# A two-layer attention trunk on one core: a second place for P of the selected branch, shared with the split G rows, and new prices in the planner that orders the second layer

## The chip, the core and the metric

The kernel runs on one core of a Trainium2 chip. Engines are named as the profile names them: PE is TensorE's matmul stream and PEld its weight loads, DVE is VectorE, ACT is ScalarE, POOL is GpSimd, SP is SyncE, which here issues nearly all DMAs. Each engine takes its own instructions in the order in which they were written, and waits for others through semaphores. The metric is the device time of one execution in microseconds.

## The reference, cut to what matters

```
x = x + swa(x)                 # layer A: 16 heads, window of 128 keys, sinks
shared K/V from x              # three branches: compressed, selected, window
q = rms(proj), z = proj        # layer B: 4 KV heads, 4 query heads in each
o_cmp = softmax(q k_cmp + bias) v_cmp
o_slc = softmax(q k_slc + bias, the 8 selected blocks of 64 keys) v_slc
o_win = softmax(q k_win + bias, window of 512 keys) v_win
G = sum over branches of o_b * silu(z_b) * sigmoid(gate_b)
out = x + G @ w_out
```

Sequence 1024, width 1024, all float32. The products with weights are made of float32r parts: an operand is split into a high part and the rest, and three products replace one.

## The kernel before, in words

Layer A takes the first 440 us, the shared K/V side, the queries and a part of z the next 500, and from about 940 us to the end runs what this text calls the second attention, written by `plan_b`. Its work is cut into 32 units: for each of four **quads** h (one KV head, four query heads) eight tiles i of 128 queries. Unit (i, h) makes, in this order, compressed scores (`sc_b`), window scores (`s_wb`, against up to 5 blocks of 128 keys) and selected scores (`s_sb`, up to i+1 blocks). DVE adds the bias to them while it copies them from PSUM into P (`p_wb`, `p_sb`) and takes row maxima, ACT takes the exponential in place, PE transposes P block by block (`pt_wb`, `pt_sb`), ACT or DVE copies each transposed block back, and PE multiplies it with V into `o_b`. One transposition of the row scales (`rt_b`) ends the softmax part of a unit; it serves below as the mark between units. The result goes to DRAM (`gdb`) and is read back, all quads of one tile, for the output rows (`gs`: high part and rest, 8 KB each for a partition), which `op` multiplies with `w_out`.

The products with V are **half-width**: they write 64 of the 128 output rows (shown as `128*64`), two of them side by side. All others are full-width.

Two kinds of product depend on nothing in the units and fill PE between their steps: z of the quads 1 to 3 (`z_b`, 127 groups of three 512-column products) and, once all quads of a tile are there, the output products (`op`, 128 such groups).

The order is not written by hand. Each step is an operation with an engine, a price in microseconds, a due time and the buffers it takes from rings of fixed depth; `Plan.run` picks the operation that could start first by its own prices, and so fixes every engine's order. A change of a price or of a ring moves instructions on all engines. A ring that an operation needs is a wait in the real kernel too: with `psl=1` there is one place for `p_sb`, so unit i+1 can put no selected scores away before the last product with V of unit i has read its P. Here are the lines that say how a half-width product is priced:

```
if (j + 1) * runs // n > j * runs // n:      # up to five blocks in a run
    last = plan.op("PE", 0.15 + 0.45 * len(js), ..., kind="half")
new = o["kind"] != kind.get(e)               # Plan.run: another kind than before
start = max(at, free) + self.change * new    # change: 0 in plan_b, 0.12 in plan_a
```

## Time and profile before

| | us |
|---|---|
| median of three runs (1549.99 to 1554.86) | 1550.21 |
| the profiled execution | 1548.54 |
| its span, first to last instruction | 1546.6 |
| PE busy | 1497.1 (97%) |
| PEld busy | 1202.2 (78%) |
| DVE busy | 949.7 (61%) |
| ACT busy | 784.3 (51%) |
| POOL busy | 335.2 (22%) |

Busy times of PE overlap, since products are pipelined: a 512-column product is shown with 0.39 us, and the next one starts 0.23 us later. What a stretch costs is read from starts, not from durations.

### The profile page before, as it was taken

The numbers are of one execution on the slowest core, as the hardware profiler recorded it, in microseconds if no ns is written. First come the engines' busy times: TensorE is split into PE (matmuls) and PEld (weight loads), VectorE is DVE, ScalarE is ACT, GpSimd is POOL, SyncE is SP. The second block draws the span as 40 slices with busy tenths as digits, with TensorE's granted clock in tenths as the row PEclk, the third lists the DMA queues.
The fourth block names the chain that finished last, engine by engine and source line by source line (L and its number), as shares of the span: only waits on it lengthen the run. The fifth ranks groups of instructions, "written<-read, shape, count | busy, mean of one in ns | idle before, by whom it ended". The sixth has DMA issues, their size and how long they took to land.

```text
span 1546.6 us, 26037 instructions
## 1 busy us (share of the span) xinstructions
PE 1497.1 (97%) x8579; PEld 1202.2 (78%) x8579; DVE 949.7 (61%) x3801; ACT 784.3 (51%) x1874; POOL 335.2 (22%) x417
## 2 busy tenths in 40 slices
PE   7999989999989999999999999999999999999999
PEld 5778867677768888898788887777787787668777
DVE  7678625857646544588524428875887786777431
ACT  6322315867525343242423427776777786766530
POOL 1233101211101000234100002332332342353200
PEclk9999999999999999999999999999999999999999
DMA  6365685644345323454825534334324333453132
GB/s 211 103 198 137 176 223 156 205 127 150 118 159 156 105 79 112 129 144 112 222 78 153 142 97 116 111 102 141 114 84 147 109 105 105 148 154 97 32 128 87
DMA packets 194506, 203.87 MB, mean 132 GB/s; under 512 B 22095, under 2 KB 154914, under 8 KB 194372
## 3 DMA queue, kind: packets, MB, share of 16 engines
q1 hardware_dynamic: 172368, 189.50, 41.5%
q10 hardware_dynamic: 21124, 10.49, 2.4%
q0 software_dynamic: 880, 2.23, 0.5%
q8 instruction: 68, 1.11, 0.3%
q14 instruction: 66, 0.54, 0.1%
HBM read 147.41 MB, written 56.85 MB: 132 GB/s over the span
## 4 chain that ended last, share of the span: by engine, by line
PE 80%; DVE 7%; DMA 7%; issue 2%; ACT 2%; POOL 1%; SPq 0%; POOLq 0%; DVEq 0%; ACTq 0%
PE o_b L962 7%; PE bkv L366 5%; PE pt_sb L953 4%; PE s_sb L1641 4%; PE op L864 4%; PE op L866 4%; PE op L865 4%; PE z_b L435 3%; PE z_b L434 3%; PE z_b L433 3%; PE s_wb L1641 3%; PE c L366 3%; PE pt_wb L953 3%; PE akv L366 2%; PE z_b L724 2%
## 5 line engine op out<-in xcount | busy, mean ns | idle before, releaser
L1016 ACT ACTIVATE p_sb<-p_sb,negm_sb 128x128 f32<-128x128 f32 (+7 forms) x128 | 98.8, 774 | 10.8 <-DVE negm_sb L1678 10.0
L1016 ACT ACTIVATE p_wb<-p_wb,negm_wb 128x640 f32<-128x640 f32 (+4 forms) x128 | 88.7, 695 | 21.9 <-DVE negm_wb L1678 21.2
L957 ACT COPY p_sb<-pt_sb 128x512 f32<-128x512 f32 x143 | 78.1, 587 | 41.9 <-PE pt_sb L953 41.5
L1641 PE MATMUL s_sb<-k,q_b 128*128 128x384 f32 (+3 forms) x384 | 96.6, 367 | 2.5 <-DVE mx_sb L1669 1.7
L435 PE MATMUL z_b<-xt_b,w_bz 128*128 128x512 f32 x240 | 93.9, 391 | 0.0
L434 PE MATMUL z_b<-xt_b,w_bz 128*128 128x512 f32 x240 | 93.8, 391 | 0.0
L433 PE MATMUL z_b<-xt_b,w_bz 128*128 128x512 f32 x240 | 93.7, 390 | 0.0
L673 DVE SCALAR_TENSOR_TENSOR zt_b<-zt_b,z_b 128x512 f32<-128x512 f32 x48 | 32.8, 685 | 93.9 <-ACT zt_b L670 93.8
L366 PE MATMUL bkv<-w_bkv,xt_b 128*128 128x512 f32 x336 | 85.8, 409 | 4.3 <-ACT w_bkv L315 2.8
L1641 PE MATMUL s_wb<-k,q_b 128*128 128x384 f32 (+3 forms) x384 | 85.6, 333 | 3.2 <-issue 2.7
L957 ACT COPY p_wb<-pt_wb 128x512 f32<-128x512 f32 x120 | 67.9, 582 | 35.6 <-PE pt_wb L953 34.8
L1006 POOL TENSOR_TENSOR uz_b<-uz_b,rb_b 128x512 f32<-128x512 f32 x32 | 42.0, 1312 | 198.0 <-DMA rb_b<-rdb 164.3
L953 PE MATMUL pt_sb<-consts,p_sb 128*128 128x128 f32 x576 | 79.8, 275 | 1.7 <-ACT p_sb L957 1.1
L953 PEld LDWEIGHTS pt_sb<-consts,p_sb 128*128 128x128 f32 x576 | 65.4, 141 | 17.7 <-issue 10.0
L366 PEld LDWEIGHTS bkv<-w_bkv,xt_b 128*128 128x128 f32 x336 | 64.5, 196 | 18.8 <-ACT w_bkv L315 3.2
L670 ACT ACTIVATE zt_b<-z_b 128x512 f32<-128x512 f32 x48 | 28.5, 596 | 91.7 <-PE z_b L435 72.6
L1006 POOL TENSOR_TENSOR uz_a<-uz_a,rb_a 128x256 f32<-128x256 f32 x32 | 26.0, 813 | 224.5 <-DMA rb_a<-rda 179.6
L1016 ACT ACTIVATE p_a<-p_a,negm_a 128x256 f32<-128x256 f32 (+1 forms) x128 | 61.8, 484 | 25.2 <-DVE negm_a L1257 15.2
L875 DVE TENSOR_TENSOR xo<-op,xo 128x512 f32<-128x512 f32 x32 | 22.1, 689 | 85.3 <-PE op L866 82.5
L962 PE MATMUL o_b<-p_sb,v 128*64 128x256 f32 x576 | 72.8, 390 | 0.0
L1660 DVE CUSTOM_DVE_ANT_1 p_sb<-s_sb,sel_b 128x256 f32<-128x256 f32 (+3 forms) x128 | 56.6, 453 | 25.0 <-PE s_sb L1641 18.7
L1641 PEld LDWEIGHTS s_sb<-k,q_b 128*128 128x128 f32 x384 | 62.5, 191 | 11.1 <-issue 3.6
(377 smaller groups left out, 4332.1 us busy)
## 6 DMA issues: line engine op xcount, KB each, us to landing
ws_bz<-in_b_w_in_dram SPq DMA_DIRECT2D x24, 512.0 KB
uz_b<-uzb SPq DMA_DIRECT2D x32, 384.0 KB
qda<-qs_aq SPq DMA_DIRECT2D x64, 128.0 KB
q_a<-qda SPq DMA_DIRECT2D x32, 256.0 KB
qdb<-qs_bq SPq DMA_DIRECT2D x64, 128.0 KB
q_b<-qdb SPq DMA_DIRECT2D x32, 256.0 KB
rb_b<-rdb SPq DMA_DIRECT2D x64, 128.0 KB
uzb<-zt_b ACTq DMA_DIRECT2D x30, 256.0 KB
```

What stands on the lines that cost most here:

```text
L366: mm(c["ps"], x, w(z, k), start=start and n == 0, stop=stop and n == len(ops) - 1)
L433: mm(ps, wh, xh, start=(k == 0), stop=False)
L434: mm(ps, wl, xh, start=False, stop=False)
L435: mm(ps, wh, xl, start=False, stop=(k == KC - 1))
L864: mm(u["ps"], gh, wh, start=(k == 0), stop=False)
L865: mm(u["ps"], gh, wl, start=False, stop=False)
L953: nc.tensor.transpose(t[:, g * P : (g + 1) * P], p()[:, g, cols], self.ident)
L957: nc.scalar.copy(p()[:, :, cols], t) if e == "ACT" else nc.vector.tensor_copy(p()[:, :, cols], t)
L962: nc.tensor.matmul(o()[z * HD : (z + 1) * HD], v()[:, blocks[j], :], p()[:, z::2, j * P : (j + 1) * P], start=(j == 0), stop=(j == n - 1),)
L1006: nc.gpsimd.tensor_tensor(u(), u(), c["b"], op=ALU.mult)
L1016: self.nc.scalar.activation(p[:, g, :n], p[:, g, :n], AF.Exp, bias=negm[:, g : g + 1], accum_out=sums[:, g : g + 1])
L1641: nc.tensor.matmul(s["s"][:, : nbk * P], cq(g), k[:, y, (b0 + at) * P : (b0 + at + nbk) * P], start=(y == 0), stop=(y == 1),)
```

## The change

P of the selected branch gets a second ring. Units with odd i keep the old place (`psl`), units with even i take a new one (`pev`) of the same 16 KB. The room for it is the room of the two `gs` buffers: both have the tag `both` with one buffer, so the first output rows can be split only when the last even unit has used its P; the plan lists all `pev` operations ahead of the loads of the G rows. Each of the two halves of this room then holds the G rows of one tile, by turns. The ring `uz` (z and gates of a unit) grows from 2 to 3. The prices: a change between half-width and full-width costs 0.18 in both plans, a run of half-width products 0.432 for each block instead of 0.15 + 0.45, a group of z or output products 0.69 instead of 0.66, scores a little more, and an operation of another kind is held back by 0.1 (`keep`) in `plan_b`.

```
-  0.66, product(k)                                   # z and output products
+  0.69, product(k)
-  "PE", 0.15 + 0.45 * len(js), ... times(js)         # plan_pv
+  "PE", 0.432 * len(js), ... times(js)
-  plan.change, plan.keep = 0.12, 0.15                # plan_a
+  plan.change, plan.keep = 0.18, 0.15
-  a = first = plan.op("PE", n / 600.0, scores(j), ...
+  a = first = plan.op("PE", n / 530.0, scores(j), ...
-  a = plan.op("PE", 2 * nbk * 0.054, scores(g, at, nbk, s), ...
+  a = plan.op("PE", 0.025 + 2 * nbk * 0.054, scores(g, at, nbk, s), ...
-  ... uz=2, ... psl=1, zt=2, gs=2, ...               # plan_b
+  ... uz=3, ... psl=1, pev=1, zt=2, gs=2, ...
+  def even():
+      return pool.tile([P, GRP, 1024], F32, tag="both", name="p_sb", bufs=1)
+  def part(i):
+      if not parts:
+          parts["g"] = pool.tile([P, 2, 2, SLOT], F32R, tag="both", name="gs", bufs=1)
+      return parts["g"][:, i % 2]
-  far_win if b else far_sel, None if b else fop, "pw" if b else "psl", 640 if b else 1024, prio,
+  far_win if b else far_sel, None if b else fop, "pw" if b else "psl" if i % 2 else ("pev", even),
+  ends = [o for o in plan.ops if any(b["ring"] == "pev" for b in o["bufs"])]
-  lo = self.plan_split(lambda: gd[i], KC, rows, gops, [gb], [], p, f"g{i}", 2.8)
+  lo = self.plan_split(lambda: gd[i], KC, rows, gops + (place[1] if place else []), [gb], [], p, f"g{i}", 2.8)
+  plan.change, plan.keep = 0.18, 0.1                 # plan_b
```

How the order moves on PE is seen at three places. In names of rows, `o_b4_1` is unit (4, 1), `p_wb5_1` the window P of unit (5, 1), and a final xN counts equal instructions.

**First place**, quad 1, the products with V of units 4 and 5. Before:

```order
L1641 MATMUL s_wb6_1_1_0_12445<-k1_9393,q_b6_1_12032 128x256 x2
L962 MATMUL o_b4_1_12336<-p_sb4_1_12241,v0_1_9478 64x256 x10
L1870 MATMUL ptc_b5_1_12469<-consts_116,pc_b5_1_12323 128x128 x2
L1641 MATMUL s_sb5_1_0_0_12472<-k0_9392,q_b4_1_11695 128x384 x2
L1641 MATMUL s_sb5_1_0_3_12480<-k0_9392,q_b4_1_11695 128x384 x2
L1641 MATMUL s_sb5_1_1_0_12488<-k0_9392,q_b4_1_11695 128x384 x2
L953 MATMUL pt_wb5_1_0_12491<-consts_116,p_wb5_1_12177 128x128 x4
```

and now:

```order
L1822 MATMUL sc_b6_1_12502<-kc_5014,q_b6_1_11984 128x128 x4
L724 MATMUL z_b220_12160<-xt_b_1_5040,w_b221_11162 128x512
L725 MATMUL z_b220_12160<-xt_b_1_5040,w_b221_11162 128x512
L726 MATMUL z_b220_12160<-xt_b_1_5040,w_b221_11162 128x512
L963 MATMUL o_b4_1_12517<-p_wb4_1_11993,v1_1_9471 64x256 x10
L963 MATMUL o_b5_1_12536<-p_wb5_1_12288,v1_1_9471 64x256 x10
L963 MATMUL o_b4_1_12517<-p_sb_12175,v0_1_9476 64x256 x10
L954 MATMUL pt_sb5_1_0_12581<-consts_116,p_sb5_1_12415 128x128 x4
```

Three products with V that stood apart, each between full-width ones, now stand behind each other. Over the whole second attention the half-width products stood in 76 runs before and stand in 47 now, 528 products in both; behind 31 of the 76 a transposition of P followed, behind 20 of them one of the compressed branch. In layer A there are 20 runs in both.

**Second place**, the last quad, behind the mark of unit 2. Before:

```order
L988 MATMUL rt_b2_3_15538<-consts_116,r_b2_3_15364 8x128
L1641 MATMUL s_wb4_3_0_2_15546<-k1_9393,q_b4_3_15326 128x384 x2
L1641 MATMUL s_wb4_3_1_0_15551<-k1_9393,q_b4_3_15326 128x256 x2
L1641 MATMUL s_wb4_3_1_2_15558<-k1_9393,q_b4_3_15326 128x384 x2
L962 MATMUL o_b2_3_15464<-p_sb2_3_15423,v0_3_13329 64x256 x6
L953 MATMUL pt_wb3_3_0_15578<-consts_116,p_wb3_3_15340 128x128 x4
L1641 MATMUL s_sb3_3_0_0_15587<-k0_9392,q_b2_3_15000 128x512 x2
L1641 MATMUL s_sb3_3_1_0_15591<-k0_9392,q_b2_3_15000 128x512 x2
L1641 MATMUL s_sb3_3_2_0_15604<-k0_9392,q_b2_3_15000 128x512 x2
L953 MATMUL pt_wb3_3_1_15612<-consts_116,p_wb3_3_15340 128x128 x4
L953 MATMUL pt_wb3_3_2_15619<-consts_116,p_wb3_3_15340 128x128 x4
L864 MATMUL op_0_0_15628<-wo_15232,gs_0_15536 128x512
```

and now:

```order
L989 MATMUL rt_b2_3_15463<-consts_116,r_b2_3_15358 8x128
L1644 MATMUL s_wb3_3_2_0_15465<-k1_9393,q_b2_3_14890 128x512 x2
L1644 MATMUL s_wb3_3_3_0_15474<-k1_9393,q_b2_3_14890 128x512 x2
L1887 MATMUL ptc_b3_3_15481<-consts_116,pc_b3_3_15393 128x128 x2
L1644 MATMUL s_sb3_3_0_0_15484<-k0_9392,q_b2_3_14890 128x512 x2
L724 MATMUL z_b320_15237<-xt_b_1_5040,w_b321_14226 128x512
L725 MATMUL z_b320_15237<-xt_b_1_5040,w_b321_14226 128x512
L726 MATMUL z_b320_15237<-xt_b_1_5040,w_b321_14226 128x512
L1644 MATMUL s_sb3_3_1_0_15498<-k0_9392,q_b2_3_14890 128x512 x2
L1644 MATMUL s_sb3_3_2_0_15508<-k0_9392,q_b2_3_14890 128x512 x2
L724 MATMUL z_b320_15237<-xt_b_1_5040,w_b321_14226 128x512
```

Before, z was used up in unit 0 of this quad and the first output group stood behind the mark of unit 2; now z lasts to the mark of unit 4. Counted from mark to mark, PE's order has these filling products (z and output, single instructions) in quads 0 to 3: before 162, 105, 102 and 183 (12 of z, 171 of output), now 159, 75, 90 and 63 (57 of z, 6 of output).

**Third place**, the last unit, where the output products begin now:

```order
L963 MATMUL o_b6_3_16401<-p_sb_16277,v0_3_13348 64x256 x6
L954 MATMUL pt_wb7_3_2_16607<-consts_116,p_wb7_3_16386 128x128 x4
L954 MATMUL pt_wb7_3_3_16615<-consts_116,p_wb7_3_16386 128x128 x4
L954 MATMUL pt_wb7_3_4_16628<-consts_116,p_wb7_3_16386 128x128 x4
L954 MATMUL pt_sb7_3_0_16633<-consts_116,p_sb7_3_16511 128x128 x4
L954 MATMUL pt_sb7_3_1_16641<-consts_116,p_sb7_3_16511 128x128 x4
L954 MATMUL pt_sb7_3_2_16648<-consts_116,p_sb7_3_16511 128x128 x4
L963 MATMUL o_b7_3_16653<-p_wb7_3_16386,v1_3_13185 64x256 x10
L954 MATMUL pt_sb7_3_3_16670<-consts_116,p_sb7_3_16511 128x128 x4
L954 MATMUL pt_sb7_3_4_16676<-consts_116,p_sb7_3_16511 128x128 x4
L865 MATMUL op_0_1_16682<-w_wo0_15045,gs_16646 128x512
```

The first row is the last product that reads P of an even unit; the first output product stands ten rows further. From the mark of unit 4 to here no filling product is left in the order (the 6 of output begin with the last row shown). Before, this stretch held 12, 18 and 75 of them.

## Rows read from the trace of the kernel before

**Rows 1.** The page, busy time of each engine and its share of the span.
```profile
PE 1497.1 (97%) x8579; PEld 1202.2 (78%) x8579; DVE 949.7 (61%) x3801; ACT 784.3 (51%) x1874; POOL 335.2 (22%) x417
PE 80%; DVE 7%; DMA 7%; issue 2%; ACT 2%; POOL 1%; SPq 0%; POOLq 0%; DVEq 0%; ACTq 0%
```

**Rows 2.** Busy us by stretch: PE, PEld, DVE, ACT, POOL; then PE's granted clock, DMA.
```profile
1060.00:1200.00 140.00, 137.09 (x950) 106.67 (x950) 103.88 (x524) 103.57 (x256) 47.16 (x66) 1.00 0.40 120
1340.00:1373.00 33.00, 28.90 (x165) 19.60 (x165) 27.88 (x127) 26.29 (x65) 21.70 (x20) 0.90 0.60 183
1411.70:1454.50 42.80, 42.80 (x306) 33.87 (x304) 31.15 (x169) 31.55 (x68) 16.19 (x24) 1.00 0.20 57
```

**Rows 3.** PE's timeline at 1340, 1386 and 1394 us: start, duration, instruction.
```profile
1340.50 0.40 PE L725 MATMUL z_b<-xt_b,w_b 128*128 128x512 f32 x1
1340.74 0.39 PE L726 MATMUL z_b<-xt_b,w_b 128*128 128x512 f32 x1
1341.06 0.65 PE L962 MATMUL o_b<-p_sb,v 128*64 128x256 f32 x4
1341.65 0.62 PE L1641 MATMUL s_wb<-k,q_b 128*128 128x384 f32 x2
...
1386.12 0.40 PE L866 MATMUL op<-wo,gs 128*128 128x512 f32 x1
1386.45 1.95 PE L962 MATMUL o_b<-p_sb,v 128*64 128x256 f32 x16
1388.33 1.09 PE L953 MATMUL pt_wb<-consts,p_wb 128*128 128x128 f32 x8
1389.18 0.48 PE L864 MATMUL op<-w_wo,gs 128*128 128x512 f32 x1
...
1390.87 1.04 PE L953 MATMUL pt_wb<-consts,p_wb 128*128 128x128 f32 x8
1391.66 0.48 PE L864 MATMUL op<-w_wo,gs 128*128 128x512 f32 x1
...
1394.37 2.38 PE L962 MATMUL o_b<-p_wb,v 128*64 128x256 f32 x20
1396.68 0.50 PE L864 MATMUL op<-w_wo,gs 128*128 128x512 f32 x1
```

**Rows 4.** PE's waits from 1340 to 1390 us: us in total, times, longest.
```profile
PE rt_b L988 <- DVE r_b L1942: 1.5, 1, 1.5
PE pt_sb L953 <- ACT p_sb L957: 1.1, 2, 0.9
PE oc_b L1880 <- ACT ptsc_b L1876: 0.8, 1, 0.8
...
PE o_b L962 <- ACT p_wb L957: 0.2, 1, 0.2
```

**Rows 5.** PE's timeline, the selected scores of the last unit.
```profile
1476.47 1.84 PE L1641 MATMUL s_sb<-k,q_b 128*128 128x512 f32 x5 [1.66 <-DVE mx_sb L1669]
```

**Rows 6.** PE's waits from 215 to 445 us, in layer A's attention.
```profile
PE rt_a L988 <- DVE p_a L957: 3.4, 3, 1.9
PE op L864 <- ACT gs L763: 2.2, 1, 2.2
```

**Rows 7.** Instructions on the tile `wo`: count, ns min/median/max, first and last start.
```profile
L763 ACT CAST wo<-ws_wo x4: 1029/1040/1046, 1346.2 to 1364.0; 128x1024 fp32r<-128x1024 f32 x4
```

**Rows 8.** Timeline, ACT and DVE, the first G rows split in the last quad.
```profile
1359.33 0.33 SPq L752 DMA_DIRECT2D ws_g<-gdb  x1
1365.86 1.06 ACT L763 CAST gs<-ws_g 128x1024 fp32r<-128x1024 f32 x1
1367.07 1.48 DVE L772 TENSOR_TENSOR gs<-ws_g,gs 128x1024 fp32r<-128x1024 f32 x1
```

**Rows 9.** PE's waits from 940 us to the end, those outside the last quad.
```profile
PE s_wb L1641 <- issue: 2.7, 1, 2.7
...
PE ptc_b L1870 <- ACT rr_b L992: 0.9, 1, 0.9
```

More of the change, by code (lines that the diff above doesn't have):

```diff
@@ L733, in plan_z @@
                 a = plan.op(
-                    "PE", 0.66, product(k), [a, ws[k // 4]], [] if k else [ob], [wbs[k // 4]] + ([ob] if k else []), prio,
+                    "PE", 0.69, product(k), [a, ws[k // 4]], [] if k else [ob], [wbs[k // 4]] + ([ob] if k else []), prio,
                     shy=self.shy,
@@ L795, in w_slot, with plan_out @@
         return get
-    def plan_out(self, pool, w, gd, x, out, gops, pes, place, prio, rank, rms=None):
+    def plan_out(self, pool, w, gd, x, out, gops, pes, wplace, prio, rank, rms=None, place=None):
         nc, plan = self.nc, self.plan
@@ L807, in switch @@
         def switch():
-            c["w"] = place.tile([P, 4, 2, SLOT], F32R, tag="xt", name="wo", bufs=1)
+            c["w"] = wplace.tile([P, 4, 2, SLOT], F32R, tag="xt", name="wo", bufs=1)
         def weights(half, q, after):
@@ L833, in rows @@
                 if "g" not in t:
-                    t["g"] = self.tile(pool, "gs", [P, 2, SLOT], f"gs_{i}", F32R)
+                    t["g"] = place[0](i) if place else self.tile(pool, "gs", [P, 2, SLOT], f"gs_{i}", F32R)
                 return t["g"]
@@ L889, in tile @@
                     use = [gb] + ([ob] if k else []) + ([wbufs[k // 2]] if half else [])
-                    a = plan.op("PE", 0.66, product(k), [a, sops[half][k // 2]], [] if k else [ob], use, p, shy=self.shy)
+                    a = plan.op("PE", 0.69, product(k), [a, sops[half][k // 2]], [] if k else [ob], use, p, shy=self.shy)
                 a = plan.op("DVE", 0.61, add, [a, xl], [], [ob, xb], p)
@@ L973, in plan_pv @@
                 last = plan.op(
-                    "PE", 0.15 + 0.45 * len(js), lambda js=js, times=times: times(js), outs + [last], [], [pb, ob] + vuse, prio,
+                    "PE", 0.432 * len(js), lambda js=js, times=times: times(js), outs + [last], [], [pb, ob] + vuse, prio,
                     kind="half",
@@ L1284, in plan_unit_a @@
             mb = plan.buf("mm")
-            a = first = plan.op("PE", n / 600.0, scores(j), [qop], [mb] + ([] if j else [pb]), [qb], prio, behind=[first])
+            a = first = plan.op("PE", n / 530.0, scores(j), [qop], [mb] + ([] if j else [pb]), [qb], prio, behind=[first])
             a = plan.op("DVE", 0.13 + n / 450.0, bias(j), [a] + ms, [], [mb, pb], prio)
@@ L1625, in plan_branch @@
         nb = i - b0 + 1
+        get = None if isinstance(tag, str) else tag[1]
+        tag = tag if get is None else tag[0]
         banks = [nb] if nb <= 4 else [nb // 2, nb - nb // 2]
@@ L1631, in start @@
         def start():
-            c["p"] = self.tile(pool, tag, [P, GRP, width], f"p_{nm}")
+            c["p"] = get() if get else self.tile(pool, tag, [P, GRP, width], f"p_{nm}")
             c["mx"] = st.tile([P, GRP, 4], F32, tag="mx4", name=f"mx_{nm}", bufs=8)
@@ L1695, in plan_branch @@
                 pieces = [m for m, (k0, k1) in enumerate(KEYS) if k0 < b0 + at + nbk and b0 + at < k1]
-                a = plan.op("PE", 2 * nbk * 0.054, scores(g, at, nbk, s), [qop] + [kops[m] for m in pieces], [mb] + new, [qb] + [kbufs[m] for m in pieces], prio, behind=[first])
+                a = plan.op("PE", 0.025 + 2 * nbk * 0.054, scores(g, at, nbk, s), [qop] + [kops[m] for m in pieces], [mb] + new, [qb] + [kbufs[m] for m in pieces], prio, behind=[first])
                 new, first = [], first or a
@@ L1717, in plan_b @@
         self.plan = plan = Plan(dict(
-            self.banks, w=self.wslots, unit=5, v0=2, v1=2, dd=1, cb=1, uz=2, xr=2, pc=1, pf=1, ns=1,
-            pt=2, rr=2, rb=1, g=2, pw=2, psl=1, zt=2, gs=2, xo=3, stage=self.stages,
+            self.banks, w=self.wslots, unit=5, v0=2, v1=2, dd=1, cb=1, uz=3, xr=2, pc=1, pf=1, ns=1,
+            pt=2, rr=2, rb=1, g=2, pw=2, psl=1, pev=1, zt=2, gs=2, xo=3, stage=self.stages,
             **{f"k{b}{m}": 1 for b in range(2) for m in range(len(KEYS))},
@@ L1731, in plan_b @@
         gops = [[] for _ in range(NT)]
+        parts = {}
+        def even():
[4 more added lines that the diff above has]
+            return parts["g"][:, i % 2]
         keys = [early.tile([P, 2, S], F32R, name=f"k{b}", bufs=1) for b in range(2)]
@@ L1739, in plan_b @@
                     self.plan_unit_b(
-                        pool, i, h, qd[h, i], pair, uzd[h, i], rd[h, i], gd[i, :, 2 * h : 2 * h + 2], gates[i], quad, keys, after
+                        pool, i, h, qd[h, i], pair, uzd[h, i], rd[h, i], gd[i, :, 2 * h : 2 * h + 2], gates[i], quad, keys, after,
+                        even,
                     )
                 )
+        ends = [o for o in plan.ops if any(b["ring"] == "pev" for b in o["bufs"])]
         self.plan_out(
             pool, a["b_w_out"][0], gd, x, out, gops, pes, x1, self.wofrom,
-            lambda i: 8 * NKV - 8.0 + i + self.late,
+            lambda i: 8 * NKV - 8.0 + i + self.late, place=(part, ends),
         )
         plan.shun = {"DVE": self.shun}
+        plan.change, plan.keep = 0.18, 0.1
         with self.tc.manual_schedule():
@@ L1785, in plan_quad_b, with plan_unit_b @@
         return c, bufs, ops
-    def plan_unit_b(self, pool, i, h, qd, pair, uzd, rd, gd, gates, quad, keys, after):
+    def plan_unit_b(self, pool, i, h, qd, pair, uzd, rd, gd, gates, quad, keys, after, even):
         nc, plan, st = self.nc, self.plan, pool
@@ L1921, in plan_unit_b @@
                 bufs["dd"] if b or i < 4 else nb, ops["dd"] if b or i < 4 else nsop,
-                far_win if b else far_sel, None if b else fop, "pw" if b else "psl", 640 if b else 1024, prio,
+                far_win if b else far_sel, None if b else fop, "pw" if b else "psl" if i % 2 else ("pev", even),
+                640 if b else 1024, prio,
             )
```

## The prediction

> **What bounds the kernel now.** Start with the page: PE's products are busy for 97% of the span, DVE for 61%, ACT for 51%, and the chain that ended last runs on PE for 80% [rows 1]. So time is won only where PE does less, or stops waiting. How full PE really is must be read by stretch, since busy durations overlap. In quad 1, with z products between the steps of the units, PE is busy for 137.1 of 140 us, DVE for 103.9, ACT for 103.6 [rows 2]. The stretch from 1340 to 1373 us is another thing: PE busy 28.9 of 33 us, and its granted clock is 0.90 [rows 2]. There z has just run out and no output product is ready; the waits of that place, eight rows of the list from 1.5 down to 0.2 us, add up to 5.3 us, all for ACT, DVE or POOL [rows 4]. Later in the same quad, with output products between the steps, units 5 and 6 keep PE busy for 42.8 of 42.8 us [rows 2]. So a stretch with filling products costs what PE's instructions cost, and a stretch without them costs more.
>
> Next, what one run of half-width products costs PE beside the products themselves, from starts. A run of 4 rows takes 1341.65 - 1341.06 = 0.59 us to the next start, one of 20 takes 2.31; the slope is 1.72 / 16 = 0.1075 us for each, and what is left over is 0.16 us for the run [rows 3]. The start of the first half-width product stands 0.32 to 0.33 us behind a 512-column product that elsewhere takes 0.24, so 0.09 more. And eight transpositions right behind a run take 0.85 us where eight others take 0.79, so 0.06 more [rows 3]. Together a run costs 0.16 + 0.09 + 0.06 = **0.31 us**.
>
> **The change, part by part.** The sum is made against the profiled execution, 1548.54 us, which lies 1.67 under the median of the runs, 1550.21; I add that at the end.
>
> *Fewer runs.* 76 runs become 47, the products themselves stay 528 (first place). 29 x 0.31 = **-9.0 us**. The bounds: 29 x 0.25 = 7.3 if only what lies in front of and in the run counts, and nothing at all if PE would have waited there anyway (a rival below). The Trainium skill speaks of such changes: TensorEngine Tiling (Array Packing), section Key Properties, says that a change of tiling mode drains TensorE, and TensorE: Matmul & The Clock Gate, section Step-by-step, puts the drain at about 128 cycles, 53 ns at 2.4 GHz. An estimate from those two, two drains for a run, would be 0.11 us and 3.1 us for the 29, and the sum would come out 5.9 us later. The rows show the larger cost, so I go by them.
>
> *The starved stretch is filled.* z now lasts to the mark of unit 4 of the last quad (second place), so units 1 to 4 have 9 to 18 filling products each, as in the other quads. What goes is the 5.3 us of waits [rows 4] and what the half clock took: 0.90 over 33 us is a loss of 3.3 us [rows 2]. Of these 8.6 us I leave 0.4, as covered units wait now and then too [rows 9]: **-8.2 us**. The bounds are 0 (small units wait whatever lies between them) and 8.6.
>
> *P in two places.* In the last unit PE waits 1.66 us in front of its selected scores, whose bank DVE has not yet emptied, because P of unit 6 still holds the one place [rows 5]. With two places the scores of unit 7 stand ahead of the last products with V of unit 6: **-1.6 us**.
>
> *A new starved stretch.* The 171 output products that filled units 3 to 7 of the last quad go behind the units. As PE work they only move (0.23 us each, before or after), and so do their ten instructions for a tile on other engines: three loads and two stores on SP, a cast on ACT, a rest on DVE or POOL, two additions on DVE; in the tail ACT and DVE have little else to do, and a tile gives PE 11 us. But units 5 to 7 now run bare. What is their limit? Units 5 and 6 took 42.8 us with 30 filling products of 0.23 us each, 7.0 us; without them PE has 35.8 us of work, ACT 31.55, DVE 31.15 [rows 2]. Unit 7 adds about 18 us, so PE has 54 us of work in the stretch and ACT about 47. On top come four casts of the output weights, 1.04 us each on ACT [rows 7], which stood in the old starved stretch and now stand in unit 5: ACT comes to 51.5 of 54 us. PE is still the longest, but queues in strict order, filled to 95%, will wait for each other. One bound is 0, the covered units. The other is the old starved stretch, read by its weight loads, which don't overlap: PEld is busy for 33.87 of 42.80 us where PE never waits, a share of 0.79, and for 19.60 of 33 us there [rows 2]. That is the work of 19.60 / 0.79 = 24.8 us, so 8.2 were lost, 0.33 of the work; times 54, 17.8 us. These units are larger, and their P has two places, so I go nearer to the covered row: **+7.0 us**.
>
> *The first G rows.* They are cast when the last even P is read. Then 1.06 us on ACT and 1.23 to 1.48 on DVE follow [rows 8], while PE has eight times four transpositions (about 0.4 us each) and a run of ten pairs (2.3 us): 5.5 us of cover (third place). Their load doesn't wait for P in the kernel itself, but on SP it stands behind the reading back of unit 6's scales; from issue to cast it took 6.5 us before, with a busy ACT in it [rows 8]. I take 0, and 5 us as the upper bound.
>
> *Layer A.* The prices move its order too, with 20 runs in both. Two waits of its attention could go, 3.4 and 2.2 us [rows 6], and since z and output products are now mixed where the first of them stands, I take **-1.0 us**, with bounds -5.6 and +3. `uz=3` and the other prices bring no work; quads 0 to 2 have two single waits, 2.7 and 0.9 us [rows 9], that may go or come again: 0, with 3 us to either side.
>
> The sum: 1548.54 - 9.0 - 8.2 - 1.6 + 7.0 - 1.0 = 1535.7; with the 1.67 us to the median, **1537 us**.
>
> **The rivals.** What a measurement here can tell from no change is about 0.3%, 4.7 us.
>
> *The saving turns into waits* (0.19). 45 filling products (10 us) leave quads 0 to 2 and go to quad 3, and DVE and ACT have as much to do as before in less time: in quad 1, 104 us in 140 - 7 - 3 = 130. If each run saved is waited for instead, 9.0 and the 1.0 of layer A come back: 1547 us. For it: the products with V stand later, so P and the banks of `o_b` are held longer. Against it: 80% is still far from full.
>
> *Small units stay slow* (0.12). If units 1 to 4 of the last quad wait in spite of their filling products, 8.2 us are not won: 1545.5 us. Against it: the same units in the other quads, with 6 to 18 filling products, hardly wait [rows 9].
>
> *The starved stretch only moves, and grows* (0.11). Place: units 5 to 7 of the last quad. It loses 0.33 of its work, 17.8 us; the first G rows come 5 us late; and as PE waits for those too, the output products begin at half the clock, 3.3 us. 26.1 in place of 7.0: 1556.5 us, slower. It decides the sign from 24.5 us on (1537.4 - 7.0 + 24.5 = 1554.9). For it: the row at 1340, and ACT's 95%. The Trainium skill speaks for it as well: Perfetto Trace Analysis, section Optimization Strategy, advises to interleave stages with different limits, and this change takes such an interleaving apart. By that rule alone the time would be that of this rival; no row here shows large units without filling products.
>
> **How the numbers follow.** The forecast, 1537 us, has 0.58, with a range of its own from 1529 (no loss in the bare units) to 1544 (a loss of 14). The first two rivals end at 1545.5 to 1547, at or just past the bound of no change (1545.5); I count 0.11 of their 0.31 as faster. Faster is thus 0.69, slower the last rival and a little of the first, 0.12, and no change 0.19. The range leaves out 2 in 10, the last rival and the lower end of layer A: 1529 to 1550.
>
> **What would show it.** Runs of half-width products in the second attention: 47, each still 0.25 to 0.35 us dearer than its products. At the beginning of the last quad no waits of a microsecond and a full clock. PE's waits, if any, in the 54 us ahead of the first output product, for ACT (`p_sb`, `p_wb`) and DVE, a few tenths each and 7 us in all. Then some 88 us of output products without a gap. Quad 1, with 30 filling products less, should take some 7 to 10 us less from its first mark to its last. The prediction is wrong if the bare units lose over 14 us or a half clock stands there, if the waits of quads 0 to 2 grow by several microseconds, or if layer A ends more than 3 us later.

## The result, and the profile after

The changed kernel takes 1539.38 us (median of four runs, 1535.27 to 1542.40) against 1550.55 us before: a ratio of 0.9921, 95% interval 0.9900 to 0.9941. It is 11.2 us faster by the medians; the forecast was 1537. The profiled execution is the slowest of its four, 1542.4 us, so it shows a gain of only 6.1 us over the profiled one of before. Below, terms are sized from this pair of profiles, and verdicts are taken from the medians.

The page of the changed kernel, busy times and the chain's shares, as in [rows 1]:

```profile
PE 1491.3 (97%) x8579; PEld 1208.8 (78%) x8579; DVE 961.0 (62%) x3810; ACT 776.0 (50%) x1869; POOL 323.8 (21%) x413
PE 76%; DMA 10%; DVE 7%; ACT 2%; issue 2%; POOL 1%; SPq 1%; ACTq 0%; POOLq 0%; DVEq 0%
```

The page says nothing about why: its shares hardly move (PE 80 to 76%, DMA 7 to 10%). The busy times by stretch do. The columns are those of [rows 2]; the cuts are the first compressed scores (at 920 us; the second attention is counted from there, and not from the 940 named at the start), the marks that end quads 0, 1 and 2, the mark of unit 4 of the last quad, the mark of its unit 7, and the end. The kernel before (the last two rows are the last quad up to the mark of unit 7):

```profile
920.20:1066.50 146.30, 144.39 (x960) 113.17 (x958) 114.85 (x557) 108.80 (x272) 45.80 (x64) 1.00 0.42 123
1066.50:1199.90 133.40, 130.49 (x901) 101.44 (x898) 100.96 (x506) 97.85 (x238) 45.93 (x64) 1.00 0.39 114
1199.90:1331.60 131.70, 129.63 (x896) 101.00 (x894) 98.50 (x497) 97.39 (x233) 48.16 (x65) 1.00 0.37 111
1331.60:1411.70 80.10, 74.32 (x457) 55.51 (x455) 55.81 (x256) 51.25 (x122) 37.26 (x38) 0.96 0.46 142
1411.70:1491.00 79.30, 77.42 (x502) 59.51 (x500) 42.48 (x206) 45.97 (x92) 18.93 (x27) 1.00 0.24 72
```

The changed kernel, with the output products behind the units as a sixth row:

```profile
921.30:1069.10 147.80, 142.59 (x948) 114.67 (x946) 115.16 (x570) 108.14 (x275) 45.11 (x64) 0.99 0.41 118
1069.10:1195.10 126.00, 122.50 (x864) 97.97 (x863) 99.66 (x489) 92.45 (x227) 45.75 (x64) 0.99 0.41 110
1195.10:1321.20 126.10, 124.99 (x889) 100.87 (x888) 103.19 (x516) 95.77 (x238) 46.50 (x65) 1.00 0.39 114
1321.20:1381.20 60.00, 59.01 (x406) 47.81 (x405) 48.47 (x243) 46.43 (x119) 25.41 (x33) 1.00 0.37 111
1381.20:1444.60 63.40, 59.60 (x425) 44.08 (x423) 48.40 (x206) 48.00 (x95) 23.01 (x29) 0.97 0.34 104
1444.60:1536.40 91.80, 91.80 (x413) 72.83 (x410) 18.24 (x22) 7.04 (x8) 2.76 (x3) 1.00 0.33 111
```

Filling products moved between the stretches, so their lengths can't be compared. What can be is the **loss** of a stretch: its length minus PE's busy time, plus the share of the clock that was missing times the length. Units 0 to 4 of the last quad before: 80.10 - 74.32 = 5.8, and 0.04 x 80.1 = 3.2, together 9.0 us. In this way:

| loss, us | quads 0 to 2 | last quad, units 0 to 4 | units 5 to 7 | behind |
|---|---|---|---|---|
| before | 6.9 | 9.0 | 1.9 | 0.0 |
| changed | 12.6 | 1.0 | 5.7 | 0.0 |

The clock is shown to two digits, so a loss of a quad is good to some 0.7 us.

The old starved stretch is gone (-8.0), units 5 to 7 lose more (+3.8), and so do quads 0 to 2 (+5.7). From the first compressed scores to PE's last product the second attention takes 622.2 us before and 615.1 after, 7.1 less; the three losses give +1.5, so 8.6 are left for PE's own work, in which 29 runs of half-width products less are the main change. One pair of profiles bears this out to a few us only: the same remainder, the length less its losses, is 601.5 to 607.1 us in the four profiles of this text that have 76 runs, 592.3 to 600.7 in the seven with 46 to 51, and 597.1 in the one with 35.

Where quads 0 to 2 lose: PE's waits in them.

```profile
PE s_sb L1644 <- DVE g_b L1901: 3.2, 1, 3.2
PE oc_b L1897 <- DVE mx_sb L1663: 2.3, 1, 2.3
PE z_b L724 <- DVE zt_b L673: 1.4, 1, 1.4
```

Two single waits stand where one quad goes over into the next. DVE's timeline at the first of them:

```profile
1043.30 0.25 DVE L1796 MEMSET cb<- 128x228 f32 x1
1046.75 0.21 DVE L1798 COPY cb<-dd 128x64 f32<-128x64 f32 x1 [3.20 <-DMA dd<-bias]
1046.88 0.69 DVE L1663 CUSTOM_DVE_ANT_1 p_sb<-s_sb,sel_b 128x512 f32<-128x512 f32 x1
```

DVE's next step in strict order is the bias of the next quad, whose rows (`dd`, one place) have not landed. The scores behind it are not taken out of PSUM, and PE stands. DVE stood at this load in the kernel before too, up to 5.8 us at a time, and PE waited beside none of the three pieces:

```profile
DVE cb L1781 <- DMA dd<-bias: 13.4, 3, 5.8
```

The busy times after the wait of the changed kernel:

```profile
1048.00:1051.40 3.40, 3.40 (x12) 2.78 (x11) 2.42 (x11) 1.72 (x3) 0.00 (x0) 0.51 0.55 187
```

PE is busy without a gap, at a granted clock of 0.51, the lower level (1.2 GHz): 1.7 us more are lost for a wait of 2.3. The same follows the wait of 3.2.

Where units 5 to 7 lose, the timeline of three engines:

```profile
1394.60 1.04 ACT L763 CAST wo<-ws_wo 128x1024 fp32r<-128x1024 f32 x1 [2.13 <-DMA ws_wo<-in_b_w_out_dram]
1395.11 0.69 DVE L1974 TENSOR_TENSOR uz_b<-o_b,uz_b 128x512 f32<-128x512 f32 x1 [2.90 <-POOL uz_b L1007]
1396.57 0.98 PE L1644 MATMUL s_sb<-k,q_b 128*128 128x384 f32 x2 [2.70 <-DVE mx_sb L1672]
```

ACT stands at a cast of the output weights whose load is late, DVE at the close of a unit whose scales are late, PE behind DVE. The lower clock follows here too:

```profile
1396.30:1399.60 3.30, 3.03 (x12) 1.73 (x14) 3.27 (x13) 3.30 (x7) 1.90 (x2) 0.50 0.14 47
```

This is the place to which the four casts of [rows 7] have moved.

### The profile page after: what moved, and what is told of

It is laid out like the page before. It is cut to its first block, busy times and chain, and to the rows that moved or that the text cites. A ratio compares the mean times of both kernels' runs of the same rounds, so it can differ in the third digit from the quotient of the medians.

```text
span 1540.6 us, 26012 instructions
## 1 busy us (share of the span) xinstructions
PE 1491.3 (97%) x8579; PEld 1208.8 (78%) x8579; DVE 961.0 (62%) x3810; ACT 776.0 (50%) x1869; POOL 323.8 (21%) x413
## 4 chain that ended last, share of the span: by engine, by line
PE 76%; DMA 10%; DVE 7%; ACT 2%; issue 2%; POOL 1%; SPq 1%; ACTq 0%; POOLq 0%; DVEq 0%
PE o_b L963 6%; PE bkv L366 5%; PE pt_sb L954 4%; PE s_sb L1644 4%; PE op L867 3%; PE op L865 3%; PE op L866 3%; PE z_b L435 3%; PE z_b L434 3%; PE z_b L433 3%; PE s_wb L1644 3%; PE c L366 3%; PE pt_wb L954 3%; PE akv L366 2%; PE z_b L724 2%; PE z_b L726 2%
## 5 line engine op out<-in xcount | busy, mean ns | idle before, releaser
L958 ACT COPY p_wb<-pt_wb 128x512 f32<-128x512 f32 x115 | 63.6, 580 | 29.7 <-PE pt_wb L954 29.2
L1835 POOL TENSOR_TENSOR pc_b<-pc_b,mxc_b 128x256 f32<-128x256 f32 x32 | 19.6, 614 | 264.4 <-DVE mxc_b L1832 209.6
L954 PE MATMUL pt_wb<-consts,p_wb 128*128 128x128 f32 x480 | 69.5, 278 | 0.3 <-ACT p_wb L958 0.3
```

What stands on the lines that cost most here:

```text
L954: nc.tensor.transpose(t[:, g * P : (g + 1) * P], p()[:, g, cols], self.ident)
L958: nc.scalar.copy(p()[:, :, cols], t) if e == "ACT" else nc.vector.tensor_copy(p()[:, :, cols], t)
```

## The experiments

Twelve kernels, each timed in five rounds beside the kernel before, whose median was 1549.1 to 1550.5 us in them. "Loss" is as above. The expectations, written between the runs, size a loss in another way that gives more (8.2 us for the 5.7 of units 5 to 7 in the changed kernel, 13.8 for the 7.7 of run 5), so their figures are not to be compared with those below.

**1. The prices without the places** (`e1_prices`).

```
 kernel before, with all new prices of the diff, and
+  plan.change, plan.keep = 0.18, 0.0     # plan_b; no second place, uz=2
```

> The kernel before, with all new prices but without the hold-back (keep 0) and without the second place: 76 runs of half-width products as before, but z lasts to unit 6 of the last quad, and 78 output products stand in unit 7. Theory (a run costs 0.31 us, and the two starved stretches are the other two terms): nothing comes off for runs, the starved stretch at 1340 us goes (-8.2 to -9.8), no bare units: 1541 us, that is 0.6% under the kernel before and about level with the changed one. Rival (runs are nearly free, at the 0.11 us of the drain estimate or less, and filling is what pays): with the filling it has and no bare units it beats the changed kernel by the 5 us that those lose, 1534 us.

Measured: 1561.7 us, ratio 1.0076 (1.0062 to 1.0090), slower than both kernels. Neither theory had that. The split of the output weights now falls late in the last quad (1426.7 to 1442.6 us), and there ACT waits for their loads twice, 3.05 and 2.80 us:

```profile
1430.79 1.04 ACT L763 CAST wo<-ws_wo 128x1024 fp32r<-128x1024 f32 x1 [3.05 <-DMA ws_wo<-in_b_w_out_dram]
1434.91 1.04 ACT L763 CAST wo<-ws_wo 128x1024 fp32r<-128x1024 f32 x1 [2.80 <-DMA ws_wo<-in_b_w_out_dram]
```

PE's longest waits, from 1392.6 to 1484 us, stand behind these:

```profile
PE pt_wb L953 <- ACT ptsc_b L1877: 5.0, 1, 5.0
PE pt_wb L953 <- ACT p_wb L957: 3.2, 1, 3.2
```

The units 5 to 7 lose 17.9 us, in spite of 99 filling products. But none of these stands where PE waits. The last of z and the first of output in PE's order:

```profile
1423.20 0.40 PE L726 MATMUL z_b<-xt_b,w_b 128*128 128x512 f32 x1
1449.58 0.48 PE L864 MATMUL op<-w_wo,gs 128*128 128x512 f32 x1
```

So the run shows what a late cast at the head of ACT's queue costs a bare unit, and leaves open whether filling products beside it would have covered it. The weights' split can't start before z has ended, since `wo` takes the room of an operand of z: where it stands, filling by z is over. With all new prices but no hold-back there are 76 runs, so the prices did not bring the runs together either.

**2. The last quad in one place** (`e2_lastquad`).

```
-  "psl" if i % 2 else ("pev", even),
+  "psl" if i % 2 or h == NKV - 1 else ("pev", even),
```

> The changed kernel, but in the last quad all units use the old place for P, so the shared room is free for G rows from the end of quad 2 on. The plan is the same up to there; behind it 291 output products stand in units 4 to 7 instead of 6, and there are 50 runs instead of 47. Theory (bare units lose a part of their work because ACT and DVE are too full for strict queues): the 8.2 us of waits and half clock that I read in units 5 to 7 of the profiled run fall to the 3.6 that covered units had before, three runs more cost 0.9: 3.7 us under the changed kernel, 1535.7 us, and all the rest of the profile alike. Rival (it is the waits of the units themselves, whatever lies between): no gain, 1539 to 1541 us.

Measured: 1565.09 us, 1.0095 (1.0080 to 1.0110). Not 4 us faster than the changed kernel but 26 slower. PE's only listed wait behind the units:

```profile
PE op L865 <- ACT gs L763: 8.0, 1, 8.0
```

With 297 output products used ahead of the last mark (I had counted 291), 87 are left, 20 us, and they don't cover the way of the last unit's G to DRAM and back. In the changed kernel 378 do. With the lower clock that follows the wait, 13.0 us are lost behind the units. Units 0 to 4 and 5 to 7 lost 12.9 and 6.0 us, with casts of weights and G rows between their steps. Giving the units output products back in this way is no cure; as the run also takes the second place for P from them, it doesn't say what output products alone would do.

**3. The bias rows priced later** (`e3_bias`).

```
-  ops["dd"] = plan.op("SP", 0.5, load, [], [bufs["dd"]], [], prio - 1, 2.5, held=1.46)
+  ops["dd"] = plan.op("SP", 0.5, load, [], [bufs["dd"]], [], prio - 1, 5.5, held=1.46)
```

> The changed kernel with one number in the plan: the load of a quad's bias rows is given 5.5 us until it lands instead of 2.5, so the copy that reads it stands later in DVE's order. 47 runs as there, filling products in the last quad nearly as there (51 of z instead of 57). Theory (in the changed kernel DVE waits 11.2 us in three pieces for that load, and PE waits behind it for 2.3 and 3.2 us and then runs at half the clock for 3.4 us each time, a loss of 1.7 each): 5 to 9 us come off quads 0 to 2, 1532 us. Rival (DVE would wait somewhere else, as it did for the same load in the kernel before, 13.4 us, without harm to PE): no change, 1539 us within 2.

Measured: 1541.16 us, 0.9942 (0.9930 to 0.9954): no gain over the changed kernel. The edit did what it should, DVE's waits for `dd` in the second attention fell from 11.2 to 1.0 us. But two new waits came, 3.0 us in quad 2 and 2.3 in quad 1:

```profile
PE s_wb L1644 <- DVE mx_sb L1672: 3.0, 1, 3.0
PE pt_sb L954 <- ACT p_sb L958: 2.3, 1, 2.3
```

The loss of quads 0 to 2 is 14 us, no less than in the changed kernel.

**4. The places with the old prices** (`e4_places`).

```
 changed kernel, with the five prices as before, and
-  plan.change, plan.keep = 0.18, 0.1
+  plan.change, plan.keep = 0.0, 0.1
```

> The changed kernel with the old prices: both places for P, uz 3 and the hold-back of 0.1, but a change of kind, the runs, the scores and the filling products priced as before. 50 runs; z is used up in unit 0 of the last quad, so units 1 to 6 and the start of 7 run without any filling product. Theory (bare units lose 0.15 of their work, as units 5 to 7 did after the change: 8.2 of 55): units 1 to 4 hold 44 us of work, so they lose 6.5 us instead of 3.2, and three runs more cost 0.9: 1543.5 us. Rival (bare units lose the 0.33 of the old starved stretch): 44 x 0.33 = 14.4, 1551.5 us.

Measured: 1543.75 us, 0.9954 (0.9934 to 0.9973), as the theory had it. The places (with `uz=3`) and the hold-back, without the prices, bring 50 runs and more than half of the gain. The last quad, units 0 to 4 and 5 to 7, almost without filling products:

```profile
1334.80:1391.40 56.60, 54.26 (x374) 39.22 (x372) 46.38 (x234) 44.93 (x109) 32.51 (x37) 1.00 0.48 145
1391.40:1446.60 55.20, 53.40 (x391) 41.29 (x389) 42.47 (x206) 44.06 (x91) 18.88 (x27) 1.00 0.21 65
```

They lose 2.3 and 1.8 us. Bare units are not slow in themselves, although ACT is busy here for 44.1 of 55.2 us.

**5. The G rows held in the kernel before** (`e5_hold`).

```
+  ends = [o for o in plan.ops if any(b["ring"] == "psl" and b["k"] == 30 for b in o["bufs"])]
-  lo = self.plan_split(lambda: gd[i], KC, rows, gops, [gb], ...
+  lo = self.plan_split(lambda: gd[i], KC, rows, gops + ends, [gb], ...
```

> The kernel before with one more dependency: the G rows are loaded only when unit 6 of the last quad has read its P. The order of PE is that of before up to unit 1 of the last quad; from there on 171 output products go behind the units, 9 stay in unit 7. 76 runs. Theory, new (what cost time in the old starved stretch and in units with output products is the preparation of G rows in the strict queues of ACT, DVE and SP, and units without filling products lose about 0.12 of their work, as in the kernel with places and old prices, 12.1 us in the last quad): the 16.7 us that units 0 to 7 of the last quad lost fall to 12 or 13, 1546 us. Rival, the one my prediction used (units wait because nothing fills PE): seven bare units with 97 us of work lose 0.33 of it, 32 us, 1565 us; at 0.15 of it, 1548 us.

Measured: 1553.09 us, 1.0032 (1.0017 to 1.0048), 4 to 5 us slower than before. Neither fits: not 15 us slower, as lack of filling at 0.33 would have it, and not faster. The last quad:

```profile
1331.10:1396.90 65.80, 60.04 (x394) 43.10 (x392) 52.56 (x259) 49.26 (x121) 34.64 (x39) 0.97 0.41 125
1396.90:1456.80 59.90, 56.39 (x405) 42.24 (x403) 38.68 (x195) 43.76 (x88) 20.40 (x27) 1.00 0.24 69
```

Units 0 to 4 lose 7.7 us, nearly what they did, units 5 to 7 lose 3.5 in place of 1.9. The G rows were not what starved the old stretch. What still stands in it are the casts of the output weights.

**6 and 7. The price of a run** (`e6_split`, `e7_behind`). The same 68 products that add zero to `o_b`, once in the middle of a call of half-width products, once behind its last block.

```
   for j in js:
       ...                                            # the two half-width products of block j
+      if len(js) > 1 and j == js[len(js) // 2 - 1]:  # e7: j == js[-1]
+          nc.tensor.matmul(o(), self.winm[:, P:], self.winm, start=False, stop=False)
```

> The changed kernel, same order, with 68 added full-width products that add zero to o_b (zero weights, 256 columns), one in the middle of each call of half-width products that has two blocks or more. The 47 runs become 115. To be compared with the next kernel, which has the same 68 products in another place and 73 runs. Theory (0.31 us for each run): 42 x 0.31 = 13.0 us above the next kernel; against the changed kernel 68 x 0.12 = 8.2 for the added products and 68 x 0.31 = 21.1 for the runs: 1569 us. Rival (a run costs no more than the 0.11 us of the drain estimate): 4.6 us above the next kernel, 1555 us.

> The changed kernel, same order, with the same 68 full-width products, but each behind the last block of its call, where most often a full-width product follows anyway: 73 runs, 26 more than the changed kernel. Theory (0.31 us for each run): 8.2 for the products and 26 x 0.31 = 8.1 for the runs, 1556 us. Rival (0.11): 8.2 + 2.9, 1550 us.

Measured: 1578.74 us, 1.0184 (1.0161 to 1.0207), and 1565.96 us, 1.0104 (1.0080 to 1.0128). Same order, same work, 42 runs more: 12.8 us, 0.304 us for each. By the spread of their five and six executions the difference is good to 4 us either way, so a run costs 0.2 to 0.4 us. I had priced the added products at half of what they are: each shows as two instructions (x136), and with 26 runs at 0.30 they cost (1565.96 - 1539.38 - 7.9) / 68 = 0.27 us each, with what they spare in waits (below) counted in. The difference between the two kernels does not depend on it. The timeline of the split one:

```profile
1230.23 0.60 PE L963 MATMUL o_b<-p_wb,v 128*64 128x256 f32 x4
1230.76 0.70 PE L968 MATMUL o_b<-winm 128*128 128x256 f32 x2
1231.39 0.65 PE L963 MATMUL o_b<-p_wb,v 128*64 128x256 f32 x4
1231.97 0.44 PE L1891 MATMUL ptc_b<-consts,pc_b 128*128 128x128 f32 x2
```

and of the other at the same products:

```profile
1227.74 1.03 PE L963 MATMUL o_b<-p_wb,v 128*64 128x256 f32 x8
1228.70 0.70 PE L968 MATMUL o_b<-winm 128*128 128x256 f32 x2
1229.24 0.38 PE L1891 MATMUL ptc_b<-consts,pc_b 128*128 128x128 f32 x2
```

From the first product of these to the next transposition 1.74 us split and 1.50 whole: 0.24 here, before what the transposition behind a run costs more.

The two kernels show something else. PE and ACT have the order of the changed kernel, instruction for instruction, but for the added products, and yet they lose 7.2 and 8.8 us from the first compressed scores to the end where that one loses 19.3. The three quads and the units 5 to 7 of run 7:

```profile
922.40:1073.90 151.50, 149.09 (x977) 118.11 (x976) 115.39 (x570) 108.31 (x274) 45.14 (x64) 1.00 0.39 115
1073.90:1208.90 135.00, 132.30 (x899) 103.12 (x898) 99.17 (x490) 92.64 (x227) 45.93 (x64) 0.99 0.36 105
1208.90:1343.60 134.70, 133.91 (x924) 106.04 (x921) 103.74 (x515) 96.02 (x237) 46.61 (x65) 1.00 0.35 105
1407.00:1471.50 64.50, 62.98 (x445) 47.08 (x443) 48.38 (x206) 48.09 (x95) 23.02 (x29) 1.00 0.34 106
```

Quads 0 to 2 lose 7.2 us (run 6: 6.2), near the 6.9 of the kernel before and not the 12.6 of the changed one. Units 5 to 7 lose 1.5 (run 6: 1.1) in place of 5.7, with the four casts of the output weights between the same steps; ACT waits for none of their loads there. With 20 added product instructions the stretch takes 1.1 us more than in the changed kernel. So the losses of the changed kernel are not those of its order alone: with more work of PE in the same order the loads land in time, or PE still has something to do while others wait, and these runs don't tell the two apart.

**8. More hold-back** (`e8_keep`).

```
-  plan.change, plan.keep = 0.18, 0.1
+  plan.change, plan.keep = 0.18, 0.2
-  self.run = 5
+  self.run = 10
```

> The changed kernel with the hold-back of another kind at 0.2 instead of 0.1 and up to ten blocks in a call instead of five: 35 runs instead of 47, z used up at the mark of unit 1 of the last quad instead of unit 4, output rows behind the units as there. Theory, new (a run costs 0.31 us, bare units about 0.12 of their work): 12 x 0.31 = 3.7 us less, and about 85 us of bare work that lose 10 us where the last quad of the changed kernel lost 11.4: 1535 us. Rival (bare units lose 0.33 of their work): 28 us in place of 11.4, 1552 us.

Measured: 1552.41 us, 1.0022 (1.0006 to 1.0038), as the rival had it by size. But not by its mechanism: units 5 to 7, all bare, lost 0.8 us. The loss stands in units 0 to 4, where z ends and the split of the output weights stands (1348.6 to 1369.9 us):

```profile
1330.20:1399.70 69.50, 60.92 (x399) 46.01 (x398) 53.92 (x252) 50.11 (x121) 32.72 (x39) 0.93 0.39 118
```

That is 8.6 us and, at a clock of 0.93, 4.9 more. Twelve runs fewer than in the changed kernel should have paid for 3.6 of it, at 0.30; the profile doesn't show that they did, as what is left beside the losses is 597.1 us against 595.8.

**9. The output weights held** (`e9_wo`).

```
-  a = plan.op("SP", 0.0, switch, pes, [], [], prio, 0.0)
+  a = plan.op("SP", 0.0, switch, pes + place[1], [], [], prio, 0.0)
```

> The changed kernel, but the second half of the output weights (wo, four loads, four casts on ACT, four rests) is loaded only when unit 6 of the last quad has read its P. The order is that of the changed kernel up to the mark of unit 4 of the last quad. Theory (the split of wo, put between the steps of bare units, is what blocks them: at 1394.6 ACT waits 2.1 us for a load of wo, then PE waits 2.7 us and runs at half the clock for 3.4): units 5 to 7 lose about 4 us instead of 8.2, while the G rows, now loaded behind the weights, begin some 5 us later with nothing to cover them: 1540 us, with the two parts apart in the profile. Rival (bare units wait for each other whatever else stands there): they still lose 8 us, 1544 us.

Measured: 1540.53 us, 0.9948 (0.9927 to 0.9969), as the theory had it, and the two parts apart. Units 5 to 7, then the stretch behind them:

```profile
1377.70:1435.30 57.60, 57.12 (x436) 43.68 (x433) 42.64 (x202) 43.27 (x90) 23.77 (x30) 1.00 0.28 86
1435.30:1536.10 100.80, 94.32 (x402) 74.95 (x400) 23.23 (x26) 11.12 (x12) 4.25 (x3) 0.95 0.37 123
```

The bare units lose 0.5 us in place of 5.7. What is won is given back behind them, where PE waits 6.4 us for the first G rows, loaded behind the weights, and then runs at the lower clock.

**10. Rows and weights held in the kernel before** (`e10_wo`).

```
 as 5, and
-  a = plan.op("SP", 0.0, switch, pes, [], [], prio, 0.0)
+  a = plan.op("SP", 0.0, switch, pes + ends, [], [], prio, 0.0)
```

> The kernel before with G rows and the second half of the output weights both held until unit 6 of the last quad has read its P. To be compared with the run that holds the G rows alone, 1553.1 us, whose units 0 to 4 of the last quad lose 13.8 us. Theory (the split of wo between 1345 and 1364 us is what made the old starved stretch): that loss falls to 8 or less, and some 5 us are lost in front of the first output product: 1552 us, with the two parts apart in the profile. Rival (small units without filling products wait for each other, P in one place): 13.8 stay, 1558 us.

Measured: 1553.22 us, 1.0019 (1.0002 to 1.0035), as the theory had it, and the same as run 5. The last quad:

```profile
1335.80:1393.50 57.70, 55.81 (x393) 41.84 (x391) 49.54 (x257) 44.89 (x117) 28.25 (x37) 1.00 0.36 106
1393.50:1455.70 62.20, 55.22 (x395) 40.51 (x393) 42.60 (x199) 46.82 (x91) 21.08 (x27) 1.00 0.27 83
```

Units 0 to 4 lose 1.9 us, with no filling product behind unit 1, in place of 7.7 in the run that holds the G rows alone. So it was the split of the output weights, among units that had nothing else for PE, that made the old starved stretch. Units 5 to 7 now lose 7.0, with P in one place and the weights' split at their end; in run 9, with two places, 0.5. That the second place is what makes the difference was not tried alone: the two kernels also differ in prices and hold-back.

**11. Two times put later** (`e11_late`): as 3, and 3.5 us instead of 2.2 for the load of the spread scales.

```
-  a = plan.op("SP", 1.0, load, [a], [bb], [], prio, 2.2, held=0.09 * rows)
+  a = plan.op("SP", 1.0, load, [a], [bb], [], prio, 3.5, held=0.09 * rows)
```

> The changed kernel with two more honest times in the plan: 5.5 us instead of 2.5 until the bias rows land, 3.5 instead of 2.2 until the spread scales do (3.1 to 7.0 from the issue of the second of the two loads in the changed kernel). 51 runs in the second attention, 19 in layer A, z used up at the mark of unit 1 of the last quad. Theory (the single waits of 2 to 3.5 us in quads 0 to 3 come from DVE standing at a step whose load the plan thought landed, and each also costs 1.7 us of half clock): DVE's waits for these two fall from 11.2 and 6.9 us to under 3 each, and of the 36 us that units lose here in all about 8 go, less 1.2 for four runs: 1533 us. Rival (a plan that is right here is wrong elsewhere, since what lands late changes with the order): 1540 us within 3.

Measured: 1539.36 us, 0.9930 (0.9904 to 0.9956): no gain, as the rival had it. DVE's waits for the scales are off the list, those for `dd` are 5.7 us in three pieces, and others have come: the order has 51 runs, and units 0 to 4 lose 2.4. In all its profile loses 13.6 us where the changed kernel's loses 19.3, and the time is no shorter; four runs more are 1.2 us of that, and the rest is not accounted for.

**12. G rows first, weights behind them** (`e12_rows`).

```
+  first = [split(i) for i in range(2)] if place else []      # G rows of tiles 0 and 1, behind ends
   for q in range(4):
       weights(0, q, [a])                                     # wo takes its stage behind them
-  gb = plan.buf("gs")
+  gb, t = first[i][:2] if i < len(first) else (plan.buf("gs"), {})
```

> The changed kernel with the second half of the output weights held behind the units, as in the run that holds wo (1540.5 us, where units 5 to 7 lost 2.0 us and the stretch behind them 10.0, with PE's wait of 6.4 us for the first G rows), but now the G rows of the first two tiles are loaded and split ahead of those weights; their products with the first half of the weights cover the split of wo. Same order up to unit 6 of the last quad. Theory (the split of wo costs 6 to 8 us among the units and nothing behind them, if G rows come first): units 5 to 7 lose 2 to 3 us, the stretch behind them 1 to 2 in place of 10: 1532 us, under both kernels. Rival (the weights then come late for the second half of the first tile, and PE waits for those instead): 1539 us.

Measured: 1533.38 us (1528.44 to 1539.97), 0.9884 (0.9867 to 0.9901), faster than both kernels: 6 us under the changed one by the medians, with intervals that just touch. Units 5 to 7 and the stretch behind them:

```profile
1385.40:1441.80 56.40, 56.16 (x425) 43.68 (x423) 43.77 (x203) 43.26 (x90) 21.28 (x29) 1.00 0.27 85
1441.80:1533.90 92.10, 92.02 (x412) 72.75 (x411) 20.60 (x24) 11.11 (x12) 7.54 (x5) 1.00 0.40 136
```

They lose 0.2 and 0.1 us. The first halves of two tiles cover the weights.

## Why the prediction was right, and where it was not

The time fell by 11.2 us and the forecast was 13, with the right sign. Of its terms two had the right size for the right reason, two about the right size for a reason that was right only in part, one was wrong, and one can't be told.

That the median came so near is in part luck. The terms as sized from the pair of profiles, -8.6 - 8.0 + 3.8 + 5.7 and +1.1 for the later start, add up to -6.0, like the profiled executions (-6.1); the 5 us between that and the medians are not traced to a term. Two of the prediction's own signs of being wrong came up: a half clock stands in the bare units (0.50 from 1396.3 us), and the waits of quads 0 to 2 grew by several microseconds. Two of its figures don't come out of its own rows. The eight waits that make 5.3 us were read from 1340 to 1390 us; in the starved stretch itself, to 1373 us, they are 3.6. And with no loss in the bare units its sum is 1537.4 - 7.0 = 1530.4, not 1529.

**Fewer runs, -9.0: right.** What is left of the pair of profiles is 8.6 us, the profiles with 76 runs and those with about 47 stand apart by as much, and runs 6 and 7 give 0.304 us for a run against the 0.31 worked out from [rows 3]. Only from 47 runs to 35 (run 8) no gain is seen. The estimate drawn from the Trainium skill (TensorEngine Tiling (Array Packing), Key Properties, with TensorE: Matmul & The Clock Gate, Step-by-step), 0.11 us for a run, does not agree: it would have given 4.6 us between the two kernels, where 12.8 were measured. What brings the runs together is not the price of a change. With all prices but no hold-back there are 76 (run 1), with the old prices, the places and the hold-back 50 (run 4). Whether the hold-back alone would do it was not tried.

**The starved stretch, -8.2: right in size (-8.0), its reason only in part.** The prediction took units 1 to 4 to wait because nothing filled PE. Run 10 has them bare and they lose 1.9 us; run 4 has them bare and they lose 2.3. What stood in the old stretch were the casts and rests of the output weights [rows 7], each behind a load, at the heads of ACT's, DVE's and POOL's queues. The change did two things at once: z now fills these units, and as the split can only follow the last z product, it stands behind them. What filling would do with the split still among these units was not tried. Run 4 also shows that such a split can stand among small units and cost little; why it cost 5.2 us in one order (5.7 to 0.5) and 5.8 in another (7.7 to 1.9), and no more than 2.3 in that one, is open.

**Two places and bare units, -1.6 + 7.0 = +5.4: measured +3.8, its reason again only in part.** The bare units themselves are at the lower bound of 0: they lose 0.5 and 0.2 us in runs 9 and 12. The loss is the weights' split, which moved here; the prediction had counted it as four casts of work on ACT, not as a place where ACT waits for a load with everything queued behind it. But runs 6 and 7 have the same split in the same order and lose 1.1 and 1.5 us there. So the split alone doesn't make the loss either; that PE has nothing else to do, as the prediction had it, may still be a part of it. The rival by which the starved stretch moves and grows was right that it moves and wrong that it grows.

**The first G rows, 0: right.** The first output product starts at 1441.8 us, inside the last unit, and the 91.8 us behind the mark are busy to the last tenth. That output products among the units are worth having, which the Trainium skill would suggest (Perfetto Trace Analysis, Optimization Strategy: interleave stages with different limits), is not settled here. Run 2 interleaves them and takes 26 us more, 13.0 of it behind the units because too few were left to cover the last tile; but it has P in one place there, and units 5 and 6 of the kernel before kept PE busy with them throughout [rows 2].

**Layer A, -1.0: not shown.** The second attention begins at 921.3 us instead of 920.2, and kernels with the changed layer A, instruction for instruction alike, begin it anywhere between 917.0 and 926.7 (below). Of the two waits of [rows 6] one is gone and the other is 1.4 us; the longest of their stretch, which the prediction didn't list, is where it was, 5.9 us before and 5.7 now.

**Quads 0 to 2, 0 with 3 either way: the step that failed.** They lose 5.7 us more, and quad 1, which was to take 7 to 10 us less from its first mark to its last, takes 4.0 less (121.9 for 125.9). The prediction listed the two waits it saw [rows 9] and took an order with other waits to come out even. The rival by which the saving turns into waits had the right idea and had it too large: 5.7 of the 9.0. Runs 6 and 7 speak for it: with the same order and more work of PE the loss is back at 6.2 and 7.2. Run 1 speaks against its being all: with 76 runs, as before, and another order it loses 11.8 there. Where the waits come from is shown for one order (`dd`), but mending those (runs 3 and 11) brought no time, and others came.

## What to carry to other kernels

A stretch that looks starved should be asked which instruction at the head of a strict queue waits for a load, before it is given more work to hide behind; here moving four casts was worth what filling seemed to be (runs 9 and 10), and products added to PE's stream spared nearly as much waiting in the changed one (runs 6 and 7). Work that a stage needs once (its weights) belongs where its engines are idle, behind the work that can start without it. In a kernel ordered by a planner, one late load mended tends to show up as another, so a change is judged by the sum of waits over a stretch and by the median, not by the wait that went.

## What the runs showed of the hardware that was not expected

In the changed kernel three waits of PE, of 2.3 to 3.2 us, were each followed by 3.4 us at the lower of the two clock levels, although PE was busy without a gap in two of these stretches (0.51 granted from 1048.0 to 1051.4 us) and for 3.03 of 3.30 us in the third: each cost some 1.7 us more than its length. A wait of 2.3 us in run 3 was not followed by one, and one of 3.0 us there by twice as much (0.50 from 1207.2 to 1213.9 us), so the length of the wait alone does not tell.

The runs of one kernel spread by 3 to 16 us, and nine kernels whose first 4,646 PE instructions are the same reach the first compressed scores at 917.0 to 926.7 us. So part of the spread between runs is made before the part that the change is about. The first products of two of these kernels:

```profile
917.41 0.56 PE L1822 MATMUL sc_b<-kc,q_b 128*128 128x128 f32 x4
```

```profile
926.72 0.56 PE L1837 MATMUL sc_b<-kc,q_b 128*128 128x128 f32 x4
```

The first is from run 2, the second from run 12.
